# A fused two-block network on one core: gate products of the second block's mixers alternate with two convolved projections

## Chip, core and metric

The kernel runs on one core of a Trainium2 chip. The metric is the device time of one execution in microseconds. TensorE (PE) multiplies, VectorE (DVE) and ScalarE (ACT) compute elementwise and empty the accumulators (PSUM), GpSimd (POOL) takes small elementwise work and issues a few DMAs, and SyncE (SP) issues the DMAs of the weights.

## What is computed

256 tokens of width 1024 go through a first block and then through `second_block`, two layers that each have a mixer and a feed-forward part. The change touches the mixers of the second block only. One layer's mixer is, cut to what matters here:

```python
h = rmsnorm(x, norm_mix_g[l])
proj = h @ w_in[l]
(qa, ka, va, qd, kd, vd, beta_logit, decay_logit, z, gate_logit) = jnp.split(proj, offsets, axis=-1)
...
y_attn = grid_attention(qa, ka, va) @ w_o_attn[l]
qkv = jax.nn.silu(centred_depthwise_conv(jnp.concatenate([qd, kd, vd], axis=-1), dn_conv_w[l])).astype(f32)
...
o = bidir_gated_deltanet(qd, kd, vd, beta, g)
o = rmsnorm(o, dn_out_norm_g[l]) * jax.nn.silu(z.astype(f32).reshape(b, s, DN_HEADS, DN_DV))
y_dn = o.reshape(b, s, DN_V).astype(x.dtype) @ w_o_dn[l]
gates = jax.nn.sigmoid(gate_logit).reshape(b, s, N_BRANCH, D_MODEL)
mixed = gates[:, :, 0] * y_attn + gates[:, :, 1] * y_dn
x = x + (mixed @ w_out[l]).astype(x.dtype)
```

The gated delta net works in chunks of 64 tokens and in both directions: per chunk a triangular system is inverted, and then a scan carries a state from chunk to chunk.

## The kernel before

`mix2(l)` builds one mixer. The projection of h is cut into groups of columns. A group of 256 columns is a job of 1 MB of weights (`feats`), fetched by SP in one DMA (L150) into a ring of buffers (`raw`); it is multiplied in f32 as it lies (`unsplit`), 16 products of 128x256 on TensorE (L413, into PSUM tiles `mm`, or `ex` for every third group), and each product shows as two records in the trace.

- `dnfeat(g)` makes the six groups that are convolved: 2, 3 (k), 0, 1 (q), 4, 5 (v). It runs the products, then `conv` (ScalarE's first tap, L1247, and VectorE's others, L1253, all into `cT`), and a tanh for the silu.
- `delta` is a generator in stages. It prepares k, builds and inverts the triangular matrices on VectorE (L1636 to L1697, result `xo`), normalises q (L1562 to L1580), makes the gram products (L1610), which ScalarE copies (L1613) and POOL weighs (L1620). Then the **L stage**, for four pairs of heads: PE L1748, VectorE `Yc` L1750, PE L1754, and VectorE L1763 and ScalarE L1764 that write `Ma`, with copies into `L` (L1739, L1744). Then the **scan**, 16 steps: PE L1805, evacuated by VectorE L1814 and ScalarE L1815 into `xv`, PE L1818 and L1827, and from the second chunk on L1794 and L1810.
- `grid_attn` (scores L1429, exponentials `e` L1438, their transposes L253 and `eT` L1446, values L1450, `ob` L1454) runs beside all this.
- The two gates are 8 groups of plain products with a tanh each (L1358), first `m`, then `G8`. They come behind the six convolved groups. The last group of G8 is held behind the scan's last product (`s.behind(s.pv)`).
- Behind the gates come the groups of `w_o_attn` (4 jobs of 512 KB), `w_o_dn` and `w_out`. These are split into two parts ahead of their products: ScalarE casts `wh` (L185), VectorE subtracts to `wl` (L187), both asked for at a high priority (`PRIO`).

The order of the weights' DMAs is that of the job list (`jobs_mix2`). The order on the engines is set by a scheduler of the tile framework that runs a model of the engines' times over the program and its priorities; on the chip every engine then takes its instructions in that order. `cT` is two tiles of the pool `reg`, with the tags `C8` (8 KB per partition) and `C4`; `m` shares the tag `C8` with the first, and so its memory.

Names below are those of the program: `raw` weights as fetched, `xf` the f32 activations, `wh` and `wl` split weights, `sd`, `at`, `mm` and `ex` PSUM tiles.

Of the kernel before, what the change touches and what calls it, by code (L numbers as in the profile page):

```python
# [11 lines left out]
F32 = mybir.dt.float32  # L12
# [4 lines left out]
AF = mybir.ActivationFunctionType  # L17
# [2 lines left out]

D = 1024
S = 256
NT = 2
KD = D // 128
ALPHA = math.sqrt(2.0)
# [3 lines left out]
def row_bc(ap, off, n, parts=128):  # L29
    return bass.AP(tensor=ap.tensor, offset=ap.offset + off, ap=[[0, parts], [1, n]])  # L30


class Net:
# [167 lines left out]
    def w(s, n=1):  # L201
        s.fill(1)
        r = s.subs[s.n_used:s.n_used + n]
        s.subs[s.n_used:s.n_used + n] = [None] * n
        s.n_used += n
        return r if n > 1 else r[0]
# [48 lines left out]
    def setup(s):  # L255
        nc, A = s.nc, s.A
        s.ident = s.const.tile([128, 128], F32, name="ident")
        nc.gpsimd.dma_start(s.ident, A["c_ident"])
        s.xt = s.const.tile([128, NT, D], F32, name="xt")
        for tt in range(NT):  # L260
            nc.sync.dma_start(s.xt[:, tt], A["x"][0, tt * 128:tt * 128 + 128, :])

    def setup1(s):
        nc = s.nc
        s.am = s.reg.tile([128, 2560], F32, tag="AM", name="am")
        s.cmask = s.reg.tile([128, S], F32, tag="cmask", name="cmask")
        nc.vector.memset(s.cmask, 0.0)
# [17 lines left out]
    def make_xf(s, tt, src, g):  # L285

        if tt == 0 and g == 0:
            s.xf = s.const.tile([128, KD, S], F32, tag="xTh", name="xf")
        pt = s.ps([128, 4, 128], "sd")
# [70 lines left out]
    def tok_parts(s, n, K, xch, lead=0, tail=0, tags=("mm", "mm")):  # L360
# [20 lines left out]
        while base < K:  # L381
# [6 lines left out]
            prev = None  # L388
            for tt in range(NT):
                if base < K:  # L390
# [82 lines left out]
    def rope_tables(s):  # L473
        nc, A = s.nc, s.A
        pos = A["positions"]
        pi = s.sm.tile([128, NT], I32, name="pi", bufs=1)
        nc.gpsimd.dma_start(pi, pos[0].rearrange("(t p) -> p t", p=128))
        pf = s.sm.tile([128, NT], F32, name="pf1", bufs=1)
        nc.vector.tensor_copy(pf, pi)
        w = s.view("m0")  # L480
        fr = w[:, 0:16]
        nc.gpsimd.dma_start(fr, row_bc(A["c_freq"], 0, 16))
        s.rc = s.reg.tile([128, NT, 16], F32, tag="rc", name="rc")
        s.rs = s.reg.tile([128, NT, 16], F32, tag="rs", name="rs")
# [733 lines left out]
    def jobs_mix2(s, l):  # L1218
        A = s.A
        W = A["w_in_2"][l]  # L1220
        J = s.cols(W, 2304, 272)
        for g in (2, 3):
            J += s.feats(W, 768 + 256 * g, 256)
        J += s.cols(W, 0, 512) + s.cols(W, 512, 256, 1)
        J += s.cols(W, 2576, 272)
        for g in (0, 1, 4, 5):
            J += s.feats(W, 768 + 256 * g, 256)
        for g in range(4):
            J += s.feats(W, 2848 + 256 * g, 256)
        for g in range(4):  # L1230
            J += s.feats(W, 3872 + 256 * g, 256)
        J = s.unsplit(J)
        for i in range(len(J)):
            s.alt[len(s.jobs) + i] = ("xTl", "kd") if l and i in (2, 3) else ("xTl",)
        for g in range(4):
            J += s.feats(A["w_o_attn_2"][l], 256 * g, 256)
        for g in range(4):
            J += s.feats(A["w_o_dn_2"][l], 256 * g, 256)
        J += s.cols(A["w_out_2"][l], 0, 512) + s.cols(A["w_out_2"][l], 512, 512)
        s.add_jobs(J)  # L1240

    def conv(s, u, ps, cw, blk0, taps, nblk):
        nc = s.nc
        c = taps // 2
        for b in range(2):
            w = lambda k: cw[:, k * nblk + blk0 + b:k * nblk + blk0 + b + 1]
            nc.scalar.activation(u[:, b], ps[:, b], AF.Copy, scale=w(c))  # L1247
            for k in range(taps):
                o = k - c
                if o == 0:  # L1250
                    continue
                lo, hi = max(0, -o), S - max(0, o)
                nc.vector.scalar_tensor_tensor(u[:, b, lo:hi], ps[:, b, lo + o:hi + o], w(k), u[:, b, lo:hi],  # L1253
# [21 lines left out]
    def mix2(s, l):  # L1275
        nc, A = s.nc, s.A
# [30 lines left out]
        def dnfeat(g):  # L1307
            ps = s.fps()
            s.feat_group(ps, xh, xl, g in (2, 3))
            u = cT[g // 4][:, 2 * g % 8:2 * g % 8 + 2, :]  # L1310
            s.conv(u, ps, cw, 2 * g, 5, 12)
            th = s.tmp.tile([128, 2, 256], F32, tag="d0", name="th")
            nc.scalar.activation(th, u, AF.Tanh, scale=0.5)
            nc.vector.scalar_tensor_tensor(u, th, 1.0, u, op0=OP.add, op1=OP.mult)
# [12 lines left out]
        for n in (512, 256):  # L1327
            ps = s.tok_group(n, KD, xh, xl)
# [14 lines left out]
        for tt in range(NT):  # L1343
            nc.gpsimd.tensor_tensor(out=gzh[:, tt], in0=gzh[:, tt], in1=hg[:, 2:3, :].to_broadcast([128, 8, 64]),
                                    op=OP.mult)
        for g in (0, 1, 4, 5):
            dnfeat(g)
        next(dn)
        next(dn, None)
        OD = s.dn_out(gzh)  # L1350
        m = s.reg.tile([128, 8, 256], F32, tag="C8", name="m")
        G8 = s.const.tile([128, 8, 256], F32, tag="Wc", name="G8")
        for dst in (m, G8):
            for g in range(4):
                ps = s.fps()
                with s.behind(s.pv if dst is G8 and g >= 3 else None):
                    s.feat_group(ps, xh, xl)
                nc.scalar.activation(dst[:, 2 * g:2 * g + 2], ps, AF.Tanh, scale=0.5)  # L1358
        for g in range(4):
            gs = slice(2 * g, 2 * g + 2)  # L1360
            pb = s.fps()
# [612 lines left out]


# [12 lines left out]
```

## Time and profile before

| | |
|---|---|
| median of 3 runs | 2796.04 us (2795.3 to 2796.65) |
| profiled execution | 2796.07 us, its span 2794.3 us |
| granted TensorE clock, mean | 0.98 |
| PE busy | 2672.0 us, 96% |
| DVE busy | 2082.1 us, 75% |
| ACT busy | 1643.4 us, 59% |
| POOL busy | 337.6 us, 12% |
| first mixer, the part that the change touches | about 1906 to 2052 us of the span |
| second mixer, the same | about 2399 to 2533 us |

Times in rows are microseconds from the span's start. In a timeline a row is start, duration, engine, line, operation, what it writes and reads, a count, and in brackets how long the engine had stood idle before and what released it. PEclk is the granted TensorE clock as a share of full speed. A row of the chain is start, duration and what the last-ending chain of work was doing.

### The profile page before, as it was taken

The numbers are of one execution on the slowest core, as the hardware profiler recorded it, in microseconds if no ns is written. First come the engines' busy times: TensorE is split into PE (matmuls) and PEld (weight loads), VectorE is DVE, ScalarE is ACT, GpSimd is POOL, SyncE is SP. The second block draws the span as 40 slices with busy tenths as digits, with TensorE's granted clock in tenths as the row PEclk, the third lists the DMA queues.
The fourth block names the chain that finished last, engine by engine and source line by source line (L and its number), as shares of the span: only waits on it lengthen the run. The fifth ranks groups of instructions, "written<-read, shape, count | busy, mean of one in ns | idle before, by whom it ended". The sixth has DMA issues, their size and how long they took to land. (4 is left out here: it accounts for less than half of the span.)

```text
span 2794.3 us, 41248 instructions
## 1 busy us (share of the span) xinstructions
PE 2672.0 (96%) x15729; PEld 2296.2 (82%) x15729; DVE 2082.1 (75%) x3322; ACT 1643.4 (59%) x2557; POOL 337.6 (12%) x360
## 2 busy tenths in 40 slices
PE   8999999899999999999999999889999999899899
PEld 7988898788887878787787878667788987778897
DVE  6576654657689989898998988859487856947784
ACT  5464444446467777777777777625555533454553
POOL 3234000023400000000000000024210004221000
PEclk9999999999999999999999999999999999999999
DMA  7335555444769999999999999543235543314453
GB/s 219 121 121 189 181 190 173 151 136 137 243 230 355 352 349 359 360 350 339 364 350 344 342 373 345 216 134 98 77 109 180 182 166 122 103 49 140 163 190 136
DMA packets 350090, 610.31 MB, mean 218 GB/s; under 512 B 13626, under 2 KB 175752, under 8 KB 349888
## 3 DMA queue, kind: packets, MB, share of 16 engines
q1 hardware_dynamic: 347120, 601.34, 62.4%
q0 software_dynamic: 2768, 6.28, 1.0%
q8 instruction: 126, 2.06, 0.3%
q14 instruction: 76, 0.62, 0.1%
HBM read 606.56 MB, written 1.05 MB: 217 GB/s over the span
## 5 line engine op out<-in xcount | busy, mean ns | idle before, releaser
L187 DVE TENSOR_TENSOR wl<-raw,wh 128x1024 fp32r<-128x1024 f32 (+1 forms) x938 | 1131.1, 1224 | 328.9 <-ACT wh L185 308.9
L185 ACT CAST wh<-raw 128x1024 fp32r<-128x1024 f32 (+1 forms) x996 | 1028.2, 1043 | 571.2 <-PE mm L214 164.3
L213 PE MATMUL mm<-wl,xg 128*128 128x512 f32 x896 | 354.7, 396 | 1.5
L212 PE MATMUL mm<-wh,xg 128*128 128x512 f32 x896 | 353.2, 396 | 0.0
L214 PE MATMUL mm<-wh,xg 128*128 128x512 f32 x896 | 351.5, 392 | 0.0
L418 PE MATMUL mm<-xTh,wh 128*128 128x256 f32 x1096 | 313.3, 286 | 1.4 <-ACT cqn L556 1.4
L419 PE MATMUL mm<-xTl,wh 128*128 128x256 f32 x1096 | 314.2, 287 | 0.0
L420 PE MATMUL mm<-xTh,wl 128*128 128x256 f32 x1096 | 310.8, 284 | 0.2 <-DVE wl L187 0.2
L418 PEld LDWEIGHTS mm<-xTh,wh 128*128 128x128 f32 x1096 | 208.7, 191 | 3.6 <-ACT cqn L556 1.7
L420 PEld LDWEIGHTS mm<-xTh,wl 128*128 128x128 f32 x1096 | 209.0, 191 | 0.6 <-DVE wl L187 0.4
L419 PEld LDWEIGHTS mm<-xTl,wh 128*128 128x128 f32 x1096 | 207.8, 190 | 0.5
L213 PEld LDWEIGHTS mm<-wl,xg 128*128 128x128 f32 x896 | 168.3, 188 | 43.0 <-DVE wl L187 7.6
L214 PEld LDWEIGHTS mm<-wh,xg 128*128 128x128 f32 x896 | 168.4, 188 | 36.5
L212 PEld LDWEIGHTS mm<-wh,xg 128*128 128x128 f32 x896 | 168.3, 188 | 36.6
L187 POOL TENSOR_TENSOR wl<-raw,wh 128x1024 fp32r<-128x1024 f32 x58 | 142.9, 2464 | 336.0 <-ACT wh L185 326.4
L213 PE MATMUL sd<-wl,ac 128*128 128x512 f32 x448 | 175.8, 392 | 0.0
L214 PE MATMUL sd<-wh,ac 128*128 128x512 f32 x448 | 175.6, 392 | 0.0
L413 PE MATMUL mm<-xf,raw 128*128 128x256 f32 (+1 forms) x704 | 148.6, 362 | 0.0
L212 PE MATMUL sd<-wh,ac 128*128 128x512 f32 x448 | 144.0, 394 | 0.0
L413 PEld LDWEIGHTS mm<-xf,raw 128*128 128x128 f32 x704 | 119.1, 195 | 17.2 <-issue 3.7
L185 ACT CAST ww<-raw 128x1024 fp32r<-128x1024 f32 x74 | 77.5, 1047 | 86.9 <-PE mm L420 29.6
L187 DVE TENSOR_TENSOR ww<-raw,ww 128x1024 fp32r<-128x1024 f32 x74 | 90.5, 1223 | 43.2 <-ACT ww L185 42.1
(627 smaller groups left out, 5287.3 us busy)
## 6 DMA issues: line engine op xcount, KB each, us to landing
raw<-in_expert_w_dram SPq DMA_DIRECT2D x336, 1024.0 KB, 5.5
raw<-in_w_in_dram SPq DMA_DIRECT2D x74, 1024.0 KB, 5.2
raw<-in_w_up_dram SPq DMA_DIRECT2D x44, 1024.0 KB, 5.0
raw<-in_dense_w_dram SPq DMA_DIRECT2D x33, 1024.0 KB, 5.2
raw<-in_w_down_dram SPq DMA_DIRECT2D x22, 1024.0 KB, 4.8
raw<-in_w_out_dram SPq DMA_DIRECT2D x16, 1024.0 KB, 5.0
raw<-in_w_branch_diff_dram SPq DMA_DIRECT2D x8, 1024.0 KB, 5.0
raw<-in_w_ple_gate_dram SPq DMA_DIRECT2D x8, 1024.0 KB, 5.0
```

Of the source, the lines that this page charges most:

```text
L185: s.nc.scalar.copy(r[0], raw)
L187: eng.tensor_tensor(out=r[1], in0=raw, in1=r[0].bitcast(F32), op=OP.subtract)
L212: mm(out, lhsT=lh, rhs=rh, start=start, stop=False)
L213: mm(out, lhsT=lh, rhs=rl, start=False, stop=False)
L214: return mm(out, lhsT=ll, rhs=rh, start=False, stop=stop)
L413: mm(o[:, t], lhsT=h[:, kk, sl], rhs=xh[:, kk, t], start=kk == 0, stop=kk == k - 1)
L418: mm(o, lhsT=h[:, kk, sl], rhs=xh[:, kk, :], start=kk == 0, stop=False)
L419: mm(o, lhsT=h[:, kk, sl], rhs=xl[:, kk, :], start=False, stop=False)
L420: mm(o, lhsT=l[:, kk, sl], rhs=xh[:, kk, :], start=False, stop=kk == k - 1)
```

## The change

The tile `m` gets a tag of its own, `M8`, 8 KB more per partition. That makes it possible to compute a gate's group while `cT` is in use: the four groups of m alternate with the groups 0, 1, 4 and 5 of the convolution, in the program's text and in the list of jobs. The memory comes from the buffer that the framework keeps for DMA descriptors that software writes: `SCRATCH` sets it to 4096 bytes per partition, where the default is 16384.

```diff
+SCRATCH = 4096
...
-        for g in (0, 1, 4, 5):
-            J += s.feats(W, 768 + 256 * g, 256)
-        for g in range(4):
-            J += s.feats(W, 2848 + 256 * g, 256)
+        for i, g in enumerate((0, 1, 4, 5)):
+            J += s.feats(W, 768 + 256 * g, 256) + s.feats(W, 2848 + 256 * i, 256)
...
-        for g in (0, 1, 4, 5):
+        m = s.reg.tile([128, 8, 256], F32, tag="M8", name="m")
+        G8 = None
+
+        def gate(dst, g):
+            ps = s.fps()
+            with s.behind(s.pv if dst is G8 and g >= 3 else None):
+                s.feat_group(ps, xh, xl)
+            nc.scalar.activation(dst[:, 2 * g:2 * g + 2], ps, AF.Tanh, scale=0.5)
+
+        for i, g in enumerate((0, 1, 4, 5)):
             dnfeat(g)
+            gate(m, i)
         next(dn)
         next(dn, None)
         OD = s.dn_out(gzh)
-        m = s.reg.tile([128, 8, 256], F32, tag="C8", name="m")
         G8 = s.const.tile([128, 8, 256], F32, tag="Wc", name="G8")
-        for dst in (m, G8):
-            for g in range(4):
-                ps = s.fps()
-                with s.behind(s.pv if dst is G8 and g >= 3 else None):
-                    s.feat_group(ps, xh, xl)
-                nc.scalar.activation(dst[:, 2 * g:2 * g + 2], ps, AF.Tanh, scale=0.5)
+        for g in range(4):
+            gate(G8, g)
...
-    nc = _bacc.Bacc("TRN2", target_bir_lowering=False, num_devices=1)
+    nc = _bacc.Bacc("TRN2", target_bir_lowering=False, num_devices=1,
+                    dynamic_dma_scratch_size=SCRATCH)
```

The scheduler orders the engines anew. In the changed kernel the line numbers from the gates on are four higher (L1748 is L1752, L1815 is L1819), L185 is L186, L413 is L414 and L1358 is L1352.

TensorE in the second mixer, from the third pair of heads of the L stage to the scan's first product, before:

```order
L1754 MATMUL sd<-Yc,L 128x32 x4
L1748 MATMUL sd<-Wa,L 128x32 x4
L413 MATMUL ex<-xf,raw 128x256 x4
L253 MATMUL at<-ident,ob 128x128
L413 MATMUL ex<-xf,raw 128x256 x2
L413 MATMUL mm<-xf,raw 128x256 x4
L1754 MATMUL sd<-Yc,L 128x32 x4
L1748 MATMUL sd<-Wa,L 128x32 x4
L413 MATMUL mm<-xf,raw 128x256 x11
L1754 MATMUL sd<-Yc,L 128x32 x4
L1805 MATMUL sd<-xv,Ma 64x128 x4
L413 MATMUL mm<-xf,raw 128x256
```

The same engine in the changed kernel, all four pairs of heads:

```order
L1752 MATMUL sd<-Wa,L 128x32 x4
L414 MATMUL mm<-xf,raw 128x256 x8
L1758 MATMUL sd<-Yc,L 128x32 x4
L1752 MATMUL sd<-Wa,L 128x32 x4
L1758 MATMUL sd<-Yc,L 128x32 x4
L1752 MATMUL sd<-Wa,L 128x32 x4
L1758 MATMUL sd<-Yc,L 128x32 x4
L1752 MATMUL sd<-Wa,L 128x32 x4
L1758 MATMUL sd<-Yc,L 128x32 x4
L1809 MATMUL sd<-xv,Ma 64x128 x4
```

Before, gate products (L413) lie in every gap between the L stage's products, and one more behind the scan's first. Now the last eight of the third group of G8 lie in the first gap, and the other gaps are empty. The first mixer has the same pattern, with seven.

ScalarE in the second mixer, at the end of the L stage and the start of the scan, before:

```order
L1764 ACTIVATE Ma<-sd 32x2x2x32 x2
L1815 COPY xv<-sd 64x2x64
L1764 ACTIVATE Ma<-sd 32x2x2x32
L1815 COPY xv<-sd 64x2x64
L1358 ACTIVATE G_23427<-mm 128x512
L1829 COPY u<-at 128x128
L1815 COPY xv<-sd 64x2x64
L1829 COPY u<-at 128x128
L185 CAST wh<-raw 128x1024
L1815 COPY xv<-sd 64x2x64
```

And in the changed kernel, from the second of the three casts there:

```order
L186 CAST wh<-raw 128x1024
L1768 ACTIVATE Ma<-sd 32x2x2x32
L1352 ACTIVATE G_23507<-mm 128x512
L1352 ACTIVATE G_23507<-ex 128x512
L1352 ACTIVATE G_23507<-mm 128x512
L1768 ACTIVATE Ma<-sd 32x2x2x32
L186 CAST wh<-raw 128x1024
L1768 ACTIVATE Ma<-sd 32x2x2x32
L1819 COPY xv<-sd 64x2x64
L1768 ACTIVATE Ma<-sd 32x2x2x32
L1819 COPY xv<-sd 64x2x64
```

Before, the first cast of `w_o_attn` comes behind the scan's third evacuation (L1815). Now three casts, the first of them some twelve rows further up between the copies of L, come ahead of the first evacuation (L1819). In the first mixer two casts stood ahead of it before, and three do now.

## Rows read from the trace of the kernel before

**Rows 1.** The page: share of TensorE; chain by engine; the software DMA queue.
```profile
PE 2672.0 (96%) x15729; PEld 2296.2 (82%) x15729; DVE 2082.1 (75%) x3322; ACT 1643.4 (59%) x2557; POOL 337.6 (12%) x360
...
q0 software_dynamic: 2768, 6.28, 1.0%
...
PE 25%; DVE 7%; ACT 2%; DMA 1%; issue 0%; DVEq 0%; ACTq 0%
```

**Rows 2.** TensorE's timeline, first mixer, rows with a wait: first, longest, last of seven.
```profile
1908.98 0.98 PE L253 MATMUL at<-ident,e 128*128 128x128 f32 x4 [1.20 <-ACT e L1438]
...
1971.27 0.65 PE L253 MATMUL sd<-ident,cT 128*128 128x128 f32 x4 [2.48 <-ACT qkT L1580]
1972.44 0.44 PE L253 MATMUL at<-ident,e 128*128 128x128 f32 x2 [0.52 <-ACT e L1438]
```

**Rows 3.** Windows: length, busy PE, PEld, DVE, ACT, POOL; PEclk, DMA share, GB/s.
```profile
1930.00:1940.00 10.00, 8.12 (x35) 6.25 (x33) 10.00 (x18) 4.41 (x11) 0.00 (x0) 0.83 0.34 105
...
1970.00:1980.00 10.00, 8.21 (x28) 6.31 (x29) 1.85 (x6) 7.15 (x20) 4.85 (x6) 0.68 0.00 0
...
2452.00:2472.00 20.00, 18.54 (x93) 14.56 (x94) 3.36 (x11) 11.09 (x34) 10.04 (x14) 0.83 0.17 53
```

**Rows 4.** TensorE's timeline, second mixer, rows with a wait: first and last of five.
```profile
2433.05 2.42 PE L413 MATMUL ex<-xf,raw 128*128 128x256 f32 x10 [1.44 <-DVE cT L1253]
...
2454.11 0.44 PE L253 MATMUL at<-ident,e 128*128 128x128 f32 x2 [0.52 <-ACT e L1438]
```

**Rows 5.** The chain that ended last, first mixer, ahead of the scan.
```profile
2009.20 3.31 DMA raw<-in_w_o_attn_dram
...
2012.54 1.05 ACT wh L185
...
2013.62 1.23 DVE wl L187
...
2014.87 3.21 DMA raw<-in_w_o_attn_dram
```

**Rows 6.** ScalarE's timeline, first mixer, the scan's start.
```profile
2018.11 1.04 ACT L185 CAST wh<-raw 128x1024 fp32r<-128x1024 f32 x1 [2.64 <-DMA raw<-in_w_o_attn_dram]
...
2021.67 0.42 ACT L1815 COPY xv<-sd 64x128 f32<-64x128 f32 x2
...
2024.25 1.05 ACT L185 CAST wh<-raw 128x1024 fp32r<-128x1024 f32 x1
```

**Rows 7.** The chain, second mixer: two L products, the scan's first, a DMA.
```profile
2487.11 0.89 PE sd L1748 x8
...
2499.05 0.81 PE sd L1754 x8
2499.86 1.02 PE sd L1805 x8
...
2501.54 3.96 DMA raw<-in_w_o_attn_dram
```

**Rows 8.** ScalarE's timeline, second mixer: first evacuation, and three casts.
```profile
2500.92 0.26 ACT L1815 COPY xv<-sd 64x128 f32<-64x128 f32 x1 [0.44 <-DVE xv L1814]
...
2505.52 1.05 ACT L185 CAST wh<-raw 128x1024 fp32r<-128x1024 f32 x1 [0.88 <-DMA raw<-in_w_o_attn_dram]
...
2511.79 1.04 ACT L185 CAST wh<-raw 128x1024 fp32r<-128x1024 f32 x1
...
2518.07 1.04 ACT L185 CAST wh<-raw 128x1024 fp32r<-128x1024 f32 x1
```

**Rows 9.** The chain: the last L1805 of the first scan, and of the second.
```profile
2050.17 0.65 PE sd L1805 x4
...
2532.24 0.44 PE sd L1805 x4
```

**Rows 10.** The tile view of the eight DMAs of w_o_attn.
```profile
DMA to landing us min/median/max: 3.2/3.4/4.3
```

## The prediction

> **What bounds the kernel now.** I read the page first, for the share of each engine and the chain that ended last, then TensorE's timeline over the two mixers of the second block, then the chain and ScalarE's timeline where their scans begin. TensorE is busy for 96% of the span, and the chain names TensorE first by far [rows 1]. So a change is worth what it takes from, or adds to, the time in which TensorE stands still or runs at the lower clock. All edits lie in the two mixers; nothing outside has other work.
>
> In the first mixer TensorE waits seven times between 1908.98 and 1972.44; the rows show the first, the longest and the last [rows 2], and all seven (1.20, 1.24, 0.96, 1.88, 0.57, 2.48, 0.52) make 8.85 us. The granted clock falls behind the longer waits, to a mean of 0.83 and of 0.68 in two stretches of 10 us [rows 3]: of 8.12 and 8.21 busy us, 17% and 32% are lost, 1.4 + 2.6 = 4.0 us. Together 12.9 us. In the second mixer, behind the point where the orders part, five waits from 2433.05 to 2454.11 make 4.9 us (1.44, 0.20, 0.26, 2.48, 0.52; [rows 4]) and the clock of 0.83 over 2452 to 2472 costs 18.54 x 0.17 = 3.15 us [rows 3]: 8.0 us. These 20.9 us are what an order with better cover for the convolution could win. VectorE was full through the first of these stretches, 10.00 of 10 us [rows 3], and nearly idle in the next, 1.85: it is late with the inverse, and behind that with the q path.
>
> **What sets the start of the scan.** Behind the last product of the gates the ring of weights is free for the four 512 KB pieces of w_o_attn. Each goes round one loop: a DMA, a ScalarE cast (wh, L185), a VectorE subtraction (wl, L187), and only then the next DMA. In the first mixer that is 3.31, 1.05, 1.23, then the next DMA at 2014.87 [rows 5], a round of 5.67 us between the two DMAs, 5.57 between the first two casts and 6.14 between the next two [rows 6]. ScalarE takes its instructions in their order, so the second cast, which had waited 2.64 us for its DMA, and what stands behind it hold the evacuation xv (L1815): it starts at 2021.67 [rows 6]. In the second mixer the first DMA starts at 2501.54, behind the last short product of the third group of G8, and all three casts, at 2505.52, 2511.79 and 2518.07, come when the scan has begun (first ScalarE evacuation 2500.92) [rows 7, 8]. There the rounds are 6.27 and 6.28 us and cost the scan little: from ScalarE's first evacuation to the end of the last L1805 the second scan takes 2532.68 - 2500.92 = 31.8 us, with three casts inside, the first 2050.82 - 2021.67 = 29.2 us, with one [rows 6, 8, 9].
>
> **The change, part by part.** *Products.* Their number, 16 a group, and their durations stay. The four gate groups of m move from behind the convolutions to between them. What had been kept as filler for the L stage (L1748, L1754, four pairs of heads) is used up early: before, eleven gate products stand ahead of the last L1754; in the new order seven (eight in the second mixer) stand behind the first L1748 and then none. Hence the last gate product whose weights block w_o_attn ends sooner: by the L products that now come behind it, 0.81 to 0.89 us each [rows 7], five in the first mixer (4.3 us, with a few attention and gram products 6.5 us) and seven in the second, with the scan's first L1805 at 1.02 [rows 7], 7.1 us.
>
> *Waits of TensorE ahead of it.* The new order keeps the first three waits of the first mixer (3.4 us), and its products on the attention's e and ob, which must follow the same ScalarE and VectorE work, still find too little between them: I put 1.1 and 1.7 us on the two later e and 0.7 and 2.3 us on the two later ob, the size of such waits now [rows 2], and 1.4 us on the clock, 10.6 in all, a saving of 2.3 us. The bounds are 0 and 12.9. In the second mixer the wait of 1.44 us for cT and part of the 2.48 go: a saving of 2.2, bounds -1 and 8.0. I take values near the low end because attention, not convolution, releases most of the waits, and its order is not touched.
>
> *The loop ahead of the scan, first mixer.* The first DMA moves from 2009.2 to 2009.2 - 6.5 - 2.3 = 2000.4. Three casts now stand ahead of ScalarE's xv, where two stood. From the DMA to the end of the third cast: 3.34 + 5.57 + 6.14 + 1.05 = 16.1 us. Behind it come one pair of L products and one L1805 (0.9, 0.8 and 1.0 us, as in [rows 7]), the copies between them of 0.3 to 0.8 us and the hand-overs from engine to engine, together some 5.9 us. The first evacuation comes at 2022.4, against 2021.67: **+0.7 us**, taken as +0.5 since some of the tail is already done.
>
> *The loop ahead of the scan, second mixer.* The first DMA moves from 2501.5 to 2501.5 - 7.1 - 2.2 = 2492.2. ScalarE now has all three casts ahead of its first xv, and VectorE two subtractions ahead of its own. 3.98 + 6.27 + 6.28 + 1.05 and 0.5 for the Ma behind is 18.1 us: 2510.3 against 2500.9 to 2501.2, +9.1 us. The scan is then free of these casts and may run nearer to the 29.2 us of the first one than in 31.8: -2. **+7 us.** TensorE has only some 8 us of work in these 18.
>
> The landing time is the uncertain term. The eight DMAs took 3.2, 3.4 and 4.3 us at the least, the median and the most [rows 10], so with 3.4 for 3.96 in all rounds the second mixer comes out near +5.5. The Trainium skill (DMA: Bandwidth & Descriptors, "Anatomy of one DMA — SWDGE (gpsimd) path") gives 2.0 us plus the bytes over 436 GB/s, for another way of issuing than this one; for 512 KB that is, as an estimate, 3.2 us, which the fastest landing bears out and the 3.96 beside the scan does not. By it the sum would be some 2 us lower.
>
> A second place where a rule meets a row: ScalarE's xv stood 2.64 us plus the cast behind a DMA that it does not need [rows 6]. The Trainium skill (Perfetto Trace Analysis, "Tensor Engine Instruction (MATMUL, LD_WEIGHTS)") says that ScalarE and VectorE are strictly first in, first out, and this speaks against the change: a cast put early in the order is not passed. The trace agrees; without such a queue the second mixer would not lose its 7 us, and the sum would be near -2.
>
> *Costed at nothing.* The DMA scratch of 4096 bytes in place of 16384: the software queue, the one that POOL issues on, moves 2768 packets in all, 1.0% of the engines' time [rows 1]. Were its ring too small, a POOL DMA of constants would be late; those lie outside the mixers' tight places. Bound: 0 to 2 us. The order of the weight DMAs on SP: equal sizes, only their columns change. The memory of its own for m lifts a wait on the convolution tile that no row shows as reached. POOL's and SP's orders stay.
>
> **The sum.** +0.5 and +7: the profiled execution, 2796.07 us (span 2794.3 and 1.8 around it, the median of the runs is 2796.04), becomes 2803.6.
>
> **The rivals.** *B, no difference that a measurement can tell (within 0.2%, 5.6 us).* The landings are of the short kind, and half of the 20.9 us of waits goes: second mixer 7 - 1.8 - 1.5 = +3.7, first 0.5 - 4.1 = -3.6, 2796. For it: VectorE has fewer of the convolutions of q and v ahead of the inverse, and so ends it sooner. Against it: the L stage cannot begin before the gram products and POOL's work, which come later. The case reaches from 2791 to 2801.
>
> *C, faster.* The gate products, which need no VectorE work, cover every wait ahead of the L stage and hold the clock at full speed; first mixer 0.5 - 10.6 = -10, second 7 - 5.8 = +1: 2787. It decides once the saving in both mixers together is over 4.5 + 13 = 17.5 of the 20.9 us, or less where the landings are short as well. For it: the 1.44 and 2.48 us are waits on just this work. Against: most others are attention's. 2785 to 2790.
>
> *D, the change does nothing to time:* the waits move from one place to another, and the L stage takes what the early part gives. This is in B, at 2796.
>
> **How the numbers follow.** Forecast (three rounds ahead of the second scan, over 5.6 us) 0.50, at 2802 to 2811; B and D 0.34; C and what lies between it and B 0.16. The highest end takes no saving at all (+4.5) and 2 us of lower clock behind the thin L stage, 2810; the lower end takes in B and the near half of C, 2790. One run of this kernel differs from the next by 0.05%, so 0.2% is about what can be told from no change: faster 0.16, same 0.34, slower 0.50.
>
> **What would show it.** In the profile after, ScalarE's timeline of the second mixer has three casts ahead of the first xv, each behind a DMA, with idle TensorE of some 10 us ahead of L1809 (the old L1805), and the first evacuation some 9 us later than 2501; in the first mixer it is within 3 us of 2021.7. VectorE's xo (L1697) comes sooner. It would be wrong if w_o_attn's first DMA starts over 6 us sooner than I put it, or if the casts come behind the start of the scan.

## The result, and the profile after

The changed kernel took 2815.72 us (median of 6 runs, 2813.06 to 2816.68) beside 2795.55 us for the kernel before (6 runs): a ratio of 1.0072, 95% interval 1.0061 to 1.0083. That is 20.2 us slower. Slower was forecast, but by 7.5 us and at most 15. The profiled execution took 2815.04 us, its span 2813.2, clock 0.976.

The page after, with the lines that answer to [rows 1]:

```profile
PE 2677.9 (95%) x15729; PEld 2301.3 (82%) x15729; DVE 2089.4 (74%) x3322; ACT 1645.2 (58%) x2557; POOL 337.7 (12%) x360
...
q0 software_dynamic: 2768, 6.28, 1.0%
...
PE 24%; DVE 7%; DMA 2%; ACT 1%; issue 1%; ACTq 0%; DVEq 0%
```

TensorE has the same instructions and is busy 5.9 us longer: products at a lower clock. DMA has gone from 1% to 2% of the chain, in rounded shares: 1% of the span is 28 us. To see where the time lies I measure both mixers from one anchor each, TensorE's first transpose of the attention's `e` (L253, L254 after): 1908.98 and 2386.89 before, 1908.79 and 2394.56 after. All times in the next table are microseconds from the anchor, read from the timelines. "L stage" is its first product, "evac" is ScalarE's first scan evacuation, "scan end" the end of the last L1805, "O" the first transpose of the scan's result, "h" the end of the transposes that open the feed-forward part. The last column of a mixer is its length: from the first anchor to the second, and from the second to the end of the span.

| | L stage | evac | scan end | O | h | length |
|---|---|---|---|---|---|---|
| first mixer, before | 82.2 | 112.7 | 141.8 | 159.6 | 206.6 | 477.9 |
| after | 97.0 | 115.7 | 145.5 | 165.0 | 215.4 | 485.8 |
| second mixer, before | 85.9 | 114.0 | 145.8 | 165.3 | 215.9 | 407.4 |
| after | 102.1 | 123.3 | 152.2 | 177.3 | 226.0 | 418.6 |

The first mixer loses 7.9 us and the second 11.2. Of the 7.9, 3.0 are there at the evacuation, and of the 11.2, 9.3. The second scan then runs in 28.9 us instead of 31.8 and gives 2.9 back. But 4.2 and 4.8 us come behind the scans, in what I call the tails, where the text of the program was not changed.

The start of the second scan, ScalarE's timeline of the changed kernel, which answers to [rows 8]:

```profile
2504.57 1.04 ACT L186 CAST wh<-raw 128x1024 fp32r<-128x1024 f32 x1 [0.46 <-DMA raw<-in_w_o_attn_dram]
...
2510.65 1.04 ACT L186 CAST wh<-raw 128x1024 fp32r<-128x1024 f32 x1 [0.31 <-DMA raw<-in_w_o_attn_dram]
...
2516.47 1.04 ACT L186 CAST wh<-raw 128x1024 fp32r<-128x1024 f32 x1 [2.58 <-DMA raw<-in_w_o_attn_dram]
2517.53 0.27 ACT L1768 ACTIVATE Ma<-sd 32x128 f32<-32x128 f32 x1
2517.83 0.26 ACT L1819 COPY xv<-sd 64x128 f32<-64x128 f32 x1
```

All three casts stand ahead of the first xv, 6.08 and 5.82 us apart, and the third waited 2.58 us for its DMA. TensorE's timeline in the same stretch, the L stage from its second pair of heads on:

```profile
2501.85 1.06 PE L1752 MATMUL sd<-Wa,L 128*128 128x32 f32 x8
2504.09 1.08 PE L1758 MATMUL sd<-Yc,L 128*128 128x32 f32 x8 [1.19 <-DVE Yc L1754]
...
2508.09 1.89 PE L1758 MATMUL sd<-Yc,L 128*128 128x32 f32 x8 [1.87 <-DVE Yc L1754]
2509.80 1.89 PE L1752 MATMUL sd<-Wa,L 128*128 128x32 f32 x8
2513.74 1.89 PE L1758 MATMUL sd<-Yc,L 128*128 128x32 f32 x8 [2.05 <-DVE Yc L1754]
2515.56 1.97 PE L1809 MATMUL sd<-xv,Ma 128*64 128x128 f32 x8
```

Two things are seen here. TensorE waits for the small copies of VectorE, and the same eight records that took 1.06 us take 1.89 from the third pair on: the granted clock is at the lower level, 1.2 GHz, and its mean over the stretch is 0.71, and 0.74 in the first mixer (windows of the changed kernel, columns as in [rows 3]):

```profile
2005.00:2024.00 19.00, 15.60 (x89) 14.75 (x88) 10.45 (x32) 11.40 (x30) 5.71 (x7) 0.74 0.35 111
...
2497.00:2518.00 21.00, 15.85 (x90) 14.86 (x89) 10.26 (x32) 11.94 (x30) 3.61 (x5) 0.71 0.25 76
```

The second L stage of the kernel before had no wait and the full clock (windows of the kernel before):

```profile
2473.00:2501.00 28.00, 28.00 (x176) 25.23 (x176) 9.19 (x35) 11.18 (x33) 4.15 (x6) 1.00 0.13 39
```

The L stage had 36 gate products between its first and its last L product, in either mixer. In the changed kernel 7 and 8 are left there, as many as stand in its first gap; the others now stand ahead of the stage, which therefore begins 15 to 16 us later, counted from the anchor.

So two theories stand beside each other. **Loop:** the rounds of DMA, cast and subtraction ahead of the scans hold them up. **Thin L stage:** the L stage itself is slow because too little stands between its products, with casts or without. And the tails behind the scans are open.

### The profile page after: what moved, and what is told of

It is laid out like the page before. It is cut to its first block, busy times and chain, and to the rows that moved or that the text cites. A ratio compares the mean times of both kernels' runs of the same rounds, so it can differ in the third digit from the quotient of the medians.

```text
span 2813.2 us, 41253 instructions
## 1 busy us (share of the span) xinstructions
PE 2677.9 (95%) x15729; PEld 2301.3 (82%) x15729; DVE 2089.4 (74%) x3322; ACT 1645.2 (58%) x2557; POOL 337.7 (12%) x360
## 5 line engine op out<-in xcount | busy, mean ns | idle before, releaser
L186 ACT CAST wh<-raw 128x1024 fp32r<-128x1024 f32 (+1 forms) x996 | 1028.3, 1043 | 568.3 <-PE mm L215 164.0
L214 PE MATMUL sd<-wl,ac 128*128 128x512 f32 x448 | 175.7, 392 | 0.0
L414 PE MATMUL mm<-xf,raw 128*128 128x256 f32 (+1 forms) x704 | 147.7, 360 | 0.0
L414 PEld LDWEIGHTS mm<-xf,raw 128*128 128x128 f32 x704 | 118.4, 194 | 16.4 <-issue 3.3
L186 ACT CAST ww<-raw 128x1024 fp32r<-128x1024 f32 x74 | 77.5, 1047 | 90.5 <-PE mm L421 30.0
```

The source lines that it names most:

```text
L186: s.nc.scalar.copy(r[0], raw)
L214: mm(out, lhsT=lh, rhs=rl, start=False, stop=False)
L414: mm(o[:, t], lhsT=h[:, kk, sl], rhs=xh[:, kk, t], start=kk == 0, stop=kk == k - 1)
```

## The experiments

Each run is compared with runs of the kernel before on the same chip, which are named beside it. Every profiled execution is read in the table's terms; the execution ahead of the mixers varies by some 4 us from one to the next (the first anchor lies between 1905.4 and 1909.7), which the anchors take out.

**e1, the memory alone.** The kernel before, with

```diff
+SCRATCH = 4096
-        m = s.reg.tile([128, 8, 256], F32, tag="C8", name="m")
+        m = s.reg.tile([128, 8, 256], F32, tag="M8", name="m")
+                    dynamic_dma_scratch_size=SCRATCH)
```

> The kernel before with only the memory part of the change: m has a tile of its own (M8) and the DMA scratch is 4096 bytes; the order of jobs and of the program's text stays. Theory (loop): the cost is in the new order of products and casts, so this run is within 3 us of the kernel before. Rival (memory): the smaller scratch or m's new place costs, then it is slower by a good part of the 20 us, with late DMAs on POOL's queue.

Measured: 2795.98 us beside 2795.19, ratio 1.0001 (0.9992 to 1.001). The mixers are 478.2 and 406.9 long. The memory costs nothing; it is the order.

**e2, the casts out of the L stage.** The changed kernel, with

```diff
+            s.late[len(s.jobs) + len(J)] = lambda g=g: s.seen2[4 * g]
             J += s.feats(A["w_o_attn_2"][l], 256 * g, 256)
...
+            b, a = s.late.get(s.subj[i], lambda: (None, None))()
+            with s.behind(b):
+                s.nc.scalar.copy(r[0], raw)
...
+                s.seen2.append((b, a))
```

where `seen2` holds the evacuations of the scan's steps; the subtraction is put behind `a` in the same way.

> The changed kernel, with the split of the k-th piece of w_o_attn queued behind the scan's evacuations of step 1, 5, 9 and 13 on ScalarE and VectorE, in both mixers; all else is left to the scheduler. Theory (loop): the three rounds of DMA, cast and subtraction ahead of the second scan are what makes it start 9.2 us late. Without them a pair of heads takes about 3.15 us (as the second pair does now), so the scan's first ScalarE evacuation comes some 5 us sooner in the second mixer and 2 us sooner in the first; the whole 4 to 8 us faster than the changed kernel, 2808 to 2812. Rival (thin L stage): the L stage is late because nothing stands between its products and the clock falls to 1.2 GHz; then the first evacuations come within 1.5 us of the changed kernel's and the time stays at 2814 to 2818.

Measured: 2804.38 us beside 2795.19, ratio 1.0036 (1.0023 to 1.005), 11 us less than the changed kernel, more than expected. First mixer 483.1, second 411.6. The first evacuation comes at 114.4, 1.3 us sooner than in the changed kernel and 1.7 later than before. The second comes at 119.7: 3.6 us sooner than in the changed kernel, but still 5.7 later than before. TensorE's timeline of e2 in the second L stage, without any cast there:

```profile
2500.21 1.08 PE L1764 MATMUL sd<-Yc,L 128*128 128x32 f32 x8 [1.18 <-DVE Yc L1760]
2501.13 1.59 PE L1758 MATMUL sd<-Wa,L 128*128 128x32 f32 x8
2503.24 1.89 PE L1764 MATMUL sd<-Yc,L 128*128 128x32 f32 x8 [0.52 <-DVE Yc L1760]
2504.94 1.89 PE L1758 MATMUL sd<-Wa,L 128*128 128x32 f32 x8
2507.31 1.89 PE L1764 MATMUL sd<-Yc,L 128*128 128x32 f32 x8 [0.47 <-DVE Yc L1760]
2509.12 1.97 PE L1815 MATMUL sd<-xv,Ma 128*64 128x128 f32 x8
```

The clock falls all the same. So neither theory holds alone: of 9.3 us at the second evacuation, 3.6 go with the casts. The 5.7 that stay I put down to the thin L stage, which e3 and e5 test. A further 5.6 us come back behind the second scan: from its end to O 19.5 us, as before, where the changed kernel takes 25.1.

**e3, cover for the L stage.** The changed kernel, with

```diff
+            s.hold = s.Ly if g == 2 else None
             gate(G8, g)
...
+                            with s.behind(s.hold[(b * k + kk) // 4] if s.hold else None):
+                                mm(o[:, t], lhsT=h[:, kk, sl], rhs=xh[:, kk, t], start=kk == 0, stop=kk == k - 1)
```

where `Ly` holds the last product L1752 of each pair of heads.

> The changed kernel, with the 16 products of the third group of G8 kept behind the L stage's first products, four behind each pair of heads; nothing is said of the casts. The ring then comes free later, and in the second mixer all casts stand behind the scan's start again, as before the change. Theory (loop and filler): the clock stays at 2.4 GHz in the L stage, the second scan starts some 7 us sooner against the start of its mixer, and the whole is 6 to 12 us faster than the changed kernel, 2804 to 2810. Rival (tails): the larger part of the 20 us is in the order behind the scans, w_o_dn and w_out, and does not depend on the L stage: then less than 4 us come back.

Measured: 2802.82 us beside 2795.19, ratio 1.0025 (1.0015 to 1.0036). The sum is in the expected band, and the parts are not: the second mixer takes 401.5 us, 5.9 **less** than before the change, and the first 493.9, 16.0 more. In the second the L stage now looks like this, at 2.4 GHz and without a wait (TensorE's timeline of e3):

```profile
2501.21 1.06 PE L1758 MATMUL sd<-Wa,L 128*128 128x32 f32 x8
2502.11 1.97 PE L417 MATMUL mm<-xf,raw 128*128 128x256 f32 x8
2503.92 1.01 PE L1765 MATMUL sd<-Yc,L 128*128 128x32 f32 x8
2504.76 1.06 PE L1758 MATMUL sd<-Wa,L 128*128 128x32 f32 x8
```

with the windows of e3, in the first L stage and in the second:

```profile
2003.00:2024.00 21.00, 19.54 (x85) 17.48 (x85) 10.61 (x27) 10.32 (x28) 5.17 (x6) 0.63 0.26 79
...
2497.00:2514.00 17.00, 16.99 (x120) 15.11 (x116) 8.71 (x31) 11.67 (x36) 7.50 (x10) 1.00 0.10 30
```

In the second mixer the held products keep the ring, so w_o_attn comes late and its casts stand behind the scan's start. In the first, where the ring comes free behind the second group of G8, three casts (at 94.7, 101.0 and 109.7) still stand in the L stage, the clock is 0.63, and the evacuation comes at 117.4. TensorE waits there only once, and then works on at the lower clock: eight records of gate products take 3.76 us instead of 1.97 (TensorE's timeline of e3):

```profile
2007.65 1.15 PE L1765 MATMUL sd<-Yc,L 128*128 128x32 f32 x8 [1.46 <-DVE Yc L1761]
...
2010.32 3.76 PE L417 MATMUL ex<-xf,raw 128*128 128x256 f32 x8
```

So cover did not help an L stage that still had the casts in it. The evacuation is 4.7 of the 16.0 us; another 7 or so lie between the scan's end and O.

**e4, the second mixer only.** The changed kernel, with the new job order and `gate(m, i)` between the convolutions only `if l == 1`.

> The alternation in the second mixer only; the first mixer as before (m with its own memory, scratch 4096 in both). Theory: the two mixers' costs are separate and add up, as their traces show: first mixer up to the start of the second mixer +7.7 us, from there to the end +11.1 us. So this run is 10 to 12 us slower than the kernel before, 2806 to 2808, and its trace equals that of before up to about 1900 us plus the first mixer. Rival: a delay in one mixer carries over to the other's order or clock; then it differs from +11 by more than 3 us.

Measured: 2796.91 us beside 2795.19, ratio 1.0007 (0.9998 to 1.0016). The theory's 11 us did not come, and by more than 3 us, which is the rival's sign. The second mixer is 409.1 long, 1.7 more than before, not 11.2. Its text is that of the changed kernel, but the scheduler's order is not quite: ScalarE's timeline of e4

```profile
2498.97 1.05 ACT L186 CAST wh<-raw 128x1024 fp32r<-128x1024 f32 x1 [0.61 <-DMA raw<-in_w_o_attn_dram]
2503.24 0.26 ACT L1829 COPY xv<-sd 64x128 f32<-64x128 f32 x1 [0.28 <-DVE xv L1828]
2504.78 1.05 ACT L186 CAST wh<-raw 128x1024 fp32r<-128x1024 f32 x1 [1.28 <-DMA raw<-in_w_o_attn_dram]
```

has the third cast behind the first xv. The evacuation at 119.2 is that of e2, which has no cast there at all: beside the thin L stage the first two casts cost no more than can be told from these times. From scan end to O it takes 19.6 us again.

**e5, e4 with e3's cover.** The first mixer as before, the second with `hold`.

> The alternation in the second mixer only, with the third group of its G8 kept behind the L stage, four products behind each pair of heads; the first mixer as before. In e3 the second mixer, from its start to the end of the execution, took 390.3 us where the kernel before takes 396.2. Theory (each mixer pays by its own order): this run is some 5 to 7 us faster than the kernel before, 2788 to 2791. Rival (the gain in e3 came from the late start of its second mixer, after a first mixer that lost 16 us): then it is within 2 us of the kernel before.

Measured: 2789.49 us beside 2794.95, ratio 0.9981 (0.9972 to 0.999). Second mixer 403.3, first 478.3. The gain in e3 was the mixer's own. The second evacuation comes at 112.5, as in e3: 6.7 us sooner than in e4, 7.2 sooner than in e2 and 1.5 sooner than before. So the 5.7 us of e2 were the missing cover. Of e3's 7.2 us against e2, 4.6 are gained ahead of the L stage, which starts at 97.2 instead of 101.8 because the held products no longer stand in front of it, and 2.6 inside it.

**e6, one subtraction moved in the second tail.** The changed kernel, with

```diff
+            if g >= 2:
+                s.late[len(s.jobs) + len(J)] = lambda: (None, s.od)
             J += s.feats(A["w_o_dn_2"][l], 256 * g, 256)
```

where `od` is the scaling of O (L1477). What it aims at, the chain of the changed kernel behind the second scan:

```profile
2563.16 1.13 DVE wl L188
2564.31 4.04 DMA raw<-in_w_o_dn_dram
2568.45 1.05 ACT wh L186
2569.52 1.23 DVE wl L188
...
2571.10 0.66 DVE O L1477
```

> The changed kernel, with the subtractions of the third and fourth piece of w_o_dn queued behind the scaling of O on VectorE; by the order this moves one instruction, in the second mixer. Theory (the same loop behind the scan): in the changed kernel the third subtraction waits for a cast and that for a DMA of 4.04 us, while O's scaling stands behind it, and TensorE idles 4.8 us. Without it the transposes of O come 4 to 6 us sooner in the second mixer and the time is 3 to 5 us lower than the changed kernel's, 2811 to 2813. Rival (w_out's ring sets the end of the tail): the transposes come sooner, the time stays within 1.5 us of the changed kernel's.

Measured: 2815.67 us beside 2794.95, ratio 1.0072 (1.0058 to 1.0086). O comes 1.6 us sooner (175.7) and h at 225.9, where it was, and the time is that of the changed kernel, as the rival had it: my theory of this one instruction fell.

**e7, the first mixer only.** As e4, with `if l == 0`.

> The alternation in the first mixer only. Theory: the first mixer costs what it costs in the changed kernel, 7.9 us up to the start of the second, and the second mixer, in its old order, nothing: 2802 to 2805. Rival: the second mixer's order or clock suffers from the first one's; then it is over 2807.

Measured: 2804.64 us beside 2794.95, ratio 1.0036 (1.0022 to 1.005); mixers 486.2 and 408.8. The first mixer costs what it costs in the changed kernel, whatever the order of the second. Alone, the second mixer's alternation costs 1.7 us (e4) and the first's 9.7 (e7), together 11.4: nearly half of the changed kernel's 20.2 us is there only in the order that the scheduler makes of both.

**e8, e2 and e3 together.**

> The changed kernel with both: the third group of G8 kept behind the L stage's first products, and the pieces of w_o_attn split behind the scan's steps 1, 5, 9 and 13, in both mixers. Theory: with no DMA round ahead of the scans and with cover in the L stage the early alternation is free, and the tails alone are left: both scans start 1 to 3 us sooner against the start of their mixers than in the kernel before, and the time is 2792 to 2798. Rival (the first mixer's loss is in its tail, as in e3, 15 us): over 2800.

Measured: 2788.84 us beside 2794.95, ratio 0.9975 (0.9963 to 0.9986), faster than both kernels and than I had expected. Mixers 478.9 and 402.7: the gain is the second mixer's, and e5, with the alternation there alone, is as fast. Both scans start 4 us sooner than before the change (evacuations at 108.6 and 110.1), and the L stages, first and second, run at full clock, with the cover of e3 and no cast in them (windows of e8):

```profile
2003.00:2016.00 13.00, 12.99 (x91) 11.70 (x90) 6.49 (x24) 8.93 (x26) 4.23 (x6) 1.00 0.12 38
2479.00:2497.00 18.00, 17.71 (x130) 15.62 (x130) 9.46 (x34) 11.41 (x35) 9.25 (x13) 1.00 0.10 30
```

**e9, e10, e11: the first cast of w_out behind w_o_dn's.** In the changed kernel's first tail, and in the second of the kernel before, a cast of w_out waited over 5 us for its DMA ahead of casts with their data there. The edit, in the changed kernel, in e8 and in the kernel before, where `prev` is the cast split before it:

```diff
+        s.late[len(s.jobs) + len(J)] = lambda: s.prev
         J += s.cols(A["w_out_2"][l], 0, 512) + s.cols(A["w_out_2"][l], 512, 512)
```

> The changed kernel, with the first cast of w_out queued on ScalarE behind the cast of the last piece of w_o_dn that was split before it. In the changed kernel's first mixer that first cast of w_out (ww, 5.21 us of waiting for its DMA) stands ahead of the last piece of w_o_dn, which has long landed; in the kernel before it stands behind it. Theory (the same queue, a third time): the first mixer's tail, from the transposes of O to those of h, falls from 50.4 to about 47 us and the first mixer is 3 us shorter; in all 2 to 6 us faster than the changed kernel. Rival (the DMA of w_out sets the tail in either order): under 1.5 us.

> e8 with the same order of w_out's first cast. Theory: 2 to 5 us faster than e8, in the tails alone: 2784 to 2787. Rival: the tails of e8 (48.8 and 51.2 us from O to h) are set by the DMAs: within 1.5 us of e8's 2788.8.

> The kernel before with the same order of w_out's first cast; this moves casts in its second mixer only, where the first cast of w_out waited 5.29 us ahead of two that had their data. Theory: the second mixer's tail from O to h falls from 50.6 to 47 us, 2 to 4 us faster than the kernel before. Rival: under 1.5 us.

Measured: e9 2803.97 us beside 2795.55, ratio 1.0025 (1.0015 to 1.0035), 12 us less than the changed kernel; but not for the reason given. Its first tail is unchanged, 50.4 us from O to h, and the first mixer 485.8. The 9.0 us are in the second mixer (409.6), where the scheduler, as a by-product, put the third cast of w_o_attn behind the scan's first two evacuations (ScalarE's timeline of e9):

```profile
2508.85 1.04 ACT L190 CAST wh<-raw 128x1024 fp32r<-128x1024 f32 x1
2513.09 0.26 ACT L1825 COPY xv<-sd 64x128 f32<-64x128 f32 x1 [0.28 <-DVE xv L1824]
2513.88 0.26 ACT L1825 COPY xv<-sd 64x128 f32<-64x128 f32 x1 [0.53 <-DVE xv L1824]
2514.53 1.04 ACT L190 CAST wh<-raw 128x1024 fp32r<-128x1024 f32 x1 [0.40 <-DMA raw<-in_w_o_attn_dram]
```

The evacuation is at 120.5 and from scan end to O it takes 19.5 us. With e4 this is the second case of it: in the second mixer the third cast ahead of the scan goes with 2.8 to 4.1 us there and with 5.5 us behind the scan. In the first mixer of the changed kernel, of e6, e7 and e9 all three casts stand ahead of the scan as well, and from scan end to O it takes 19.5 us: the place of the cast alone does not make the long tail. e10 came to 2789.3 us beside 2795.55 (0.9978, 0.9967 to 0.9988), no faster than e8: from O to h its tails are shorter than e8's, 47.6 us for 48.8 and 48.0 for 51.2, but its second L stage starts 4.7 us later. e11 came to 2793.89 beside 2795.55 (0.999, 0.9981 to 1.0), where the second tail did fall, from 50.6 to 47.9 us, for a gain at the edge of what can be told.

## Why the prediction was right and wrong

**The waits ahead of the loop: right in the first mixer, not in the second.** I put 9.2 us on TensorE's waits in the first mixer's early part; they are 9.40, from these rows of TensorE's timeline of the changed kernel and five like them (1.21, 1.23, 0.96, 1.10, 0.29):

```profile
1946.51 0.66 PE L254 MATMUL at<-ident,e 128*128 128x128 f32 x4 [2.13 <-ACT e L1442]
...
1961.73 0.33 PE L254 MATMUL at<-ident,ob 128*128 128x128 f32 x1 [2.48 <-DVE ob L1458]
```

The first DMA of w_o_attn, forecast for 2000.4, started at 1999.86. In the second mixer the saving of 2.2 us hardly came: four waits (0.25, 1.27, 0.21, 2.98) make 4.7 us where 4.9 had stood. VectorE's xo ends 7.5 us sooner in the first mixer, as I had said, but the L stage does not start sooner by it.

**The second mixer's loop: the size right, the reason half.** Against the start of its mixer the second evacuation was to come 9.1 us later and came 9.3 later, with the three rounds I had counted. That it agrees so closely is luck: the first DMA started 106.7 us from the anchor, 1.4 later than forecast, and from there to the end of the third cast it took 16.3 us where I had 17.6. The scan was to win 2 and won 2.9. And I took the loop for the only limit. Close behind it stood the L stage without cover, worth 5.7 of the 9.3 by e2 and e5. I looked for some 10 us of idle TensorE ahead of L1809; its waits in the L stage make 5.1 (1.19, 1.87, 2.05), and the rest was slow products. The sentence that TensorE has only some 8 us of work in 18 says the stretch is thin, and no term follows from it.

**The first mixer's loop: too small.** +0.5 us was forecast, 3.0 measured, evacuation at 2024.47 for 2022.4. The third cast ended at 2014.34, 2.2 us sooner than I had it, but 10.1 us followed where I had 5.9. I had counted one pair of L products behind that cast, and there were two; and I had priced them at 0.8 to 1.0 us, as in [rows 7], where the thin stage runs them at the lower clock, at 1.88. The 2 us of lower clock that I kept for the high end of the range belonged into the sum, and were too few: reckoned as I did for [rows 3], the stage lost 15.60 x 0.26 = 4.1 us. By e2, 1.3 of the 3.0 us go with the casts and 1.7 stay without them.

**The step that failed: the tails at nothing.** The sum let all that lies behind the scans move along with them and gave no reason. They took 4.2 and 4.8 us more: 9.0 of the 11.4 us by which the difference of the two spans, 18.9, is over the 7.5 of the sum. What I had left out is that the scheduler orders the tails anew, too. In the second mixer TensorE stands still for 4.79 us ahead of the transposes of O, in a stretch in which w_o_dn goes through the same kind of loop (the chain above; TensorE's timeline of the changed kernel, from the end of the scan to O):

```profile
2551.05 3.72 PE L414 MATMUL mm<-xf,raw 128*128 128x256 f32 x16
...
2555.29 0.44 PE L1814 MATMUL at<-Sa,qkT 128*64 128x128 f32 x4
2555.56 0.45 PE L1831 MATMUL at<-xv,qk 128*64 128x64 f32 x8
...
2571.90 1.94 PE L254 MATMUL sd<-ident,O 128*128 128x128 f32 x8 [4.79 <-DVE O L1477]
```

And the same place in the kernel before, whose last L1805 ends at 2532.68:

```profile
2532.60 4.58 PE L413 MATMUL mm<-xf,raw 128*128 128x256 f32 x20
...
2537.40 0.40 PE L1810 MATMUL at<-Sa,qkT 128*64 128x128 f32 x4
2537.62 0.45 PE L1827 MATMUL at<-xv,qk 128*64 128x64 f32 x8
2538.00 2.86 PE L413 MATMUL mm<-xf,raw 128*128 128x256 f32 x12
```

In the changed kernel the scan's last products stand behind all 32 records of the last gate group and the first five of w_o_attn, and end 9.2 us behind the last L1809; before they stood behind 20 of the 32 and ended 5.4 us behind it. So the last piece of O is written 3.3 us later against the end of the scan, and its scaling then stands behind w_o_dn's subtractions on VectorE. Of all the mixers in these thirteen traces three have this order: this one, the second of e6 and the first of e3. They take 25.1, 23.7 and 25.0 us from scan end to O; the others take 17.7 to 19.6. No run moved these products alone, so that the order goes with the long tail is shown, and that it makes it is argued.

In the first mixer O's transposes now stand behind 96 records of w_o_attn instead of 81, which is the order that TensorE had in the second mixer before: from scan end to h it takes 69.9 us instead of 64.8, and there it took 70.1. Of the 5.1 us, 1.7 lie ahead of O. The 3.4 between O and h stayed in e6, e7 and e9 (3.4 to 3.6) and 2.1 of them in e2. My reason for them, the early cast of w_out, fell with e9, though the same edit shortened this stretch in e10 and e11; which instruction costs them is open.

**At nothing, and rightly:** the memory and the scratch (e1).

**The rivals.** C, the early cover winning all waits, did not come about by the change alone. With the cover and the casts set right it is there in part: e8 is 6.1 us faster than the kernel before. Whether the kernel before would gain from the same two edits without the alternation was not run. B and D, no difference, fell with the 20.2 us: the waits that were to be saved mostly stayed. Sum of the terms: +3.0 + 0.7 + 4.2 in the first mixer, +9.3 - 2.9 + 4.8 in the second, 19.1 of the 18.9 us between the two spans.

## What to carry to other kernels

Work that waits for nothing is cover, and it is worth most where a chain of small steps passes between engines; moved away from there to where TensorE is busy anyway, it is spent. When an edit frees a ring of buffers sooner, ask what its next transfers will do: here they brought casts that wait for DMAs into the queues of ScalarE and VectorE, just ahead of the chain that starts the scan, and the evacuation stood behind a cast that waited 2.58 us. Where a scheduler makes the order, a small edit moves things far from its place (e9 asked for one cast of the tails to be moved, and nearly all of the 9.0 us that it won in the second mixer lie ahead of that cast). So price what the new order does behind the place of the edit as well, and pin what matters to an instruction, in the scan and in the L stage, as e8 does.

## What the runs showed of the hardware that I had not expected

The granted clock fell to the lower level in an L stage in which TensorE never waited longer than 1.18 us at a time (e2: 1.18, 0.52, 0.47) and was busy 17.82 of 20 us, with a mean clock of 0.74:

```profile
2492.00:2512.00 20.00, 17.82 (x102) 16.79 (x100) 8.28 (x31) 10.77 (x30) 4.68 (x7) 0.74 0.08 27
```

With four products of 128x256 in every gap between the L products it stayed at 1.00 in e3's second L stage and in both of e8. In e3's first L stage, with the same four products but with the casts, it fell after the single wait of 1.46 us and stayed at the lower level while TensorE was busy without a break (windows of e3):

```profile
2009.00:2024.00 15.00, 15.00 (x56) 13.50 (x56) 5.35 (x13) 7.11 (x20) 1.90 (x2) 0.50 0.25 76
```

I had looked for the lower clock behind long waits only, as in [rows 2, 3].
